# A transformer block on one core: weight blocks of the seven-product pairs loaded along diagonals with one wide addition, and layer norm's steps four blocks at a time

## The chip, the cores and the metric

The kernel runs on one core of a Trainium2 chip. Its time is the device time of one execution in microseconds (us), the median over several runs. A core has an engine for matmuls (PE, TensorE), and beside it VectorE (DVE), ScalarE (ACT), GpSimd (POOL) and SyncE (SP), which here issues nearly all DMAs. Each engine works through a queue of its own in a fixed order; an instruction that has to wait holds up all that stand behind it on that engine.

## The reference

One layer over 256 tokens of width 4096, in float32:

```
xn   = RMSNorm(x)
q, k, v, z_a, a_c, g_c, z_c = split(xn @ w_in)          # 7 x 2048 columns
y_a  = RMSNorm(chunked_attention(q, k, v)) * silu(z_a)  # 16 heads of 128
u    = causal_depthwise_conv_31(a_c * sigmoid(g_c))
y_c  = RMSNorm(silu(layer_norm(u)) @ w_pw + b_pw) * silu(z_c)
h    = x + [y_a, y_c] @ w_out
h    = h + sigmoid(RMSNorm(h) @ w_gate + b) * (p @ w_ple)
out  = RMSNorm(h)
```

Nearly all of the work is in the products with `w_in` (4096 x 14336), `w_pw` (2048 x 2048), `w_out` and `w_gate` (4096 x 4096 each).

## The kernel before

**How a product is tiled.** A float32 product is made of three matmuls on numbers cut into a high and a low part (fp32r): high by high, low by high, high by low. Weights stream from HBM; the activations stay on the core as 128 x 128 blocks. `mixed_product` computes 256 tokens by two blocks of 512 columns. It goes over K in *pairs* of two 128-row blocks, 16 pairs for K = 4096. A plain pair takes 8 block products, so 24 matmuls of 128x512. A pair with a star in the order table (`dense`, `early`, `early_six` and so on) is a *seven-product pair*: a Strassen-like scheme with 7 block products, 21 matmuls. Call the four 128x512 weight blocks of a pair B00, B01 (upper rows, left and right column block) and B10, B11 (lower rows). The scheme needs the sums

```
ua = [B00 + B01, B01 + B11]
ub = [ua0 + B11, ua0 + B11 + B10]
```

beside the blocks B00, B01, B10, B11 themselves. There are 130 such pairs in the program.

**What each engine does for a pair.** SP issues two DMAs of 512 KB into tiles `wt`, of which there are 5 buffers; tile `w0` holds B00 and B01, tile `w1` holds B10 and B11 (L405, through `two_columns`). ACT makes the high parts: `wh` from `wt`, `uh` from `ua` and from `ub` (L204). DVE makes the low parts `wl`, `ul` (L205) and the sums: two additions of 512 elements for `ua` (L428, L429), two for `ub` (L432, L433). For a seven-product pair the low parts are `wl` of B00 alone (128x512, since B01 enters sums only), `wl` of all of `w1` (128x1024), `ul` of `ua` and `ul` of `ub` (128x1024 each). PE then takes P1 (B00), P5 and P7 (`ua`), P2 (B10), P3 (B11), P6 and P4 (`ub`), L372. The banks P2, P3, P4 and one more are called `acc`, the four others `acc_P`.

**What sets the order.** The kernel is written pair by pair; a scheduler then interleaves the instructions on each engine's queue, and every queue is fixed when the program is built. Small pieces of other work lie in a list `later`; `fill(n)` after each pair emits the next n of them. In the first half these are the taps of the convolution (`conv_tap`, L682 and L678, 496 DVE instructions of at most 128x256), then layer norm (`layer_norm_swish`): the mean, subtracting it (`center`, L760, 16 DVE instructions of 128x256), squares, the variance, scaling (L793, 16 of 128x256) with a Silu on ACT after each (L794), and cutting into high and low (L805).

**The products in order of time** in the profile: four of the convolution's input and gate with attention's first products between them (to about 860 us), the pointwise product and attention's end (about 890 to 965), the four of z_a and z_c (to about 1330), four of `w_out` (to about 1670), four of `w_gate` (to the end).

Of the kernel before, what the change touches and what calls it, by code (L numbers as in the profile page):

```python
# [10 lines left out]
F32 = mybir.dt.float32  # L11
# [5 lines left out]
P = 128  # L17
NB = 512
# [7 lines left out]
def hybrid_block(  # L26
# [71 lines left out]

    def two_columns(w, kb, col, apart):

        rows = w[kb * P : (kb + 1) * P, :]
        return bass.AP(
            tensor=rows.tensor, offset=rows.offset + col,
            ap=[list(rows.ap[0]), [apart, 2], [1, NB]],
        )

    w_first = [wpool.tile([P, 2, NB], F32, tag="w", name="wt") for _ in range(2)]
# [91 lines left out]
    def parts_of(wt, kc, tiles=None):  # L199
        if tiles is None:  # L200
            tiles = part_tiles()
        wh, wl = tiles
        made = (
            nc.scalar.copy(wh[:, :kc, :], wt[:, :kc, :]),  # L204
            nc.vector.tensor_tensor(  # L205
                wl[:, :kc, :], wt[:, :kc, :], wh[:, :kc, :].bitcast(F32), ALU.subtract
            ),
        )
        return (wh, wl), made
# [119 lines left out]
    def mixed_product(  # L329
# [67 lines left out]
        for n, (pair, seven) in enumerate(order):  # L397
# [5 lines left out]
            for k in range(2):  # L403
                wt = wpool.tile([P, 2, NB], F32, tag="w", name="wt")
                nc.sync.dma_start(wt, two_columns(w, 2 * pair + k, col, apart))  # L405
                wts.append(wt)
# [16 lines left out]
            w0, w1 = wts  # L423
# [4 lines left out]
            plus(ua[:, 0], w0[:, 0], w0[:, 1])  # L428
            plus(ua[:, 1], w0[:, 1], w1[:, 1])  # L429
            uah, ual = pair_parts(ua)  # L430
            w1h, w1l = parts_of(w1, 2)[0]
            plus(ub[:, 0], ua[:, 0], w1[:, 1])  # L432
            plus(ub[:, 1], ub[:, 0], w1[:, 0])  # L433
            ubh, ubl = pair_parts(ub)
# [296 lines left out]
    def layer_norm_swish():  # L731
# [59 lines left out]
        def swish(c, i):  # L791
            cv, b = conv[c], 4 * c + i
            nc.vector.tensor_tensor(cv[:, i, :], cv[:, i, :], st["rs"], ALU.mult)  # L793
            nc.scalar.activation(  # L794
                cv[:, i, :], cv[:, i, :], AF.Silu,
                scale=ln_g[:, b : b + 1], bias=ln_b[:, b : b + 1],
            )
# [9 lines left out]
        n = len(conv)  # L807
        rest = [lambda: None] * 4
# [487 lines left out]
```

## Time and profile before

| | us |
|---|---|
| runs | 2048.33, 2048.42, 2051.77 |
| median | 2048.42 |
| span of the profiled execution (first to last instruction) | 2049.8 |

The profile is of one more execution; no other time than its span is recorded of it. Times in the trace are us from the span's start. In a row of grouped instructions the columns after the count are busy time, mean duration of one in ns, and the idle time of the engine just before them with what ended it. In a row of windows each engine has its busy time and the number of its instructions; then follow the clock granted to TensorE (1.00 is full), the share of time that the core's 16 DMA engines were busy, and GB/s. In a timeline row the start and the duration come first and, in brackets, how long the engine sat idle before and what it waited for. Durations of neighbouring instructions overlap a little: the distance from one start to the next is what an instruction takes of the engine.

### The profile page before, as it was taken

To read this page: it belongs to the slowest core of one execution; us is meant where nothing else is said; L and a number is where in the kernel's file an instruction comes from. 1 tells how busy PE (TensorE), PEld (TensorE's weight loads), DVE (VectorE), ACT (ScalarE), POOL (GpSimd) and SP (SyncE) were. 2 spreads that over 40 slices of the span, in tenths; PEclk is the share of its full clock that TensorE was granted. 3 is DMA by queue.
4 is the path that set the end of the run, shared out by engine and by line. 5 is a ranking of instruction groups with operands and counts; after the bars stand their busy time and mean duration, and the time that the engine had idled before them with its cause. 6 is when DMAs were issued, how large, how long until landed. Compare 5 with 4: busy or idle time off the path is not lost.

```text
span 2049.8 us, 26039 instructions
## 1 busy us (share of the span) xinstructions
PE 2021.3 (99%) x9082; PEld 1652.6 (81%) x9082; DVE 1944.7 (95%) x2784; ACT 1196.2 (58%) x1543; POOL 8.1 (0%) x19
## 2 busy tenths in 40 slices
PE   9999999999899999999999999999999999999997
PEld 7888888888678888877888888888888888888876
DVE  7999999989999999988899999999999999999998
ACT  7655545655555544576565656676565666655555
POOL 0000000000000000000000000000000000000000
PEclk9999999999999999999999999999999999999998
DMA  8666666566665665754666566676666656666765
GB/s 284 195 195 205 201 192 203 166 198 184 194 187 170 200 184 184 222 164 168 196 217 206 191 218 196 217 241 208 212 200 202 205 188 209 200 219 206 235 207 178
DMA packets 153662, 412.30 MB, mean 201 GB/s; under 512 B 12974, under 2 KB 16190, under 8 KB 153530
## 3 DMA queue, kind: packets, MB, share of 16 engines
q1 hardware_dynamic: 152880, 409.80, 62.7%
q8 instruction: 71, 1.16, 0.2%
q10 hardware_dynamic: 650, 0.84, 0.1%
q14 instruction: 61, 0.50, 0.1%
HBM read 406.39 MB, written 4.19 MB: 200 GB/s over the span
## 4 chain that ended last, share of the span: by engine, by line
PE 87%; DVE 8%; issue 2%; DMA 1%; ACT 1%; SPq 0%; POOL 0%; POOLq 0%; ACTq 0%; DVEq 0%
PE acc L372 68%; PE acc_P L372 15%; DVE wl L205 3%; DVE cv L682 1%; DVE ul L205 1%; PE tmp_ps L170 1%; DMA wt<-in_w_in_dram 1%; PE acc L218 1%; DVE ub L433 0%; DVE ub L432 0%; PE tmp_ps L835 0%; PE tmp_ps L851 0%; DVE ua L428 0%; PE tmp_ps L869 0%; DVE ua L429 0%
## 5 line engine op out<-in xcount | busy, mean ns | idle before, releaser
L372 PE MATMUL acc<-wh,big_t 128*128 128x512 f32 x4196 | 1296.4, 392 | 4.0 <-DVE wh L563 1.6
L204 ACT CAST wh<-wt 128x1024 fp32r<-128x1024 f32 (+1 forms) x737 | 711.9, 977 | 552.3 <-PE acc L372 408.0
L372 PEld LDWEIGHTS acc<-wh,big_t 128*128 128x128 f32 x4196 | 784.2, 188 | 168.5 <-ACT big_t L156 2.4
L205 DVE TENSOR_TENSOR wl<-wt,wh 128x1024 fp32r<-128x1024 f32 (+1 forms) x737 | 821.0, 1125 | 32.3 <-ACT wh L204 28.9
L372 PE MATMUL acc<-wl,big_t 128*128 128x512 f32 x2098 | 804.0, 391 | 2.0 <-DVE wl L205 1.8
L372 PEld LDWEIGHTS acc<-wl,big_t 128*128 128x128 f32 x2098 | 393.0, 188 | 87.1 <-DVE wl L205 5.7
L682 DVE SCALAR_TENSOR_TENSOR cv<-uT,dw,cv 128x255 f32<-128x255 f32 (+22 forms) x480 | 213.1, 463 | 1.0
L204 ACT CAST uh<-ub 128x1024 fp32r<-128x1024 f32 x130 | 136.9, 1053 | 125.5 <-DVE ub L433 105.1
L204 ACT CAST uh<-ua 128x1024 fp32r<-128x1024 f32 x130 | 137.1, 1054 | 84.9 <-DVE ua L429 79.6
L205 DVE TENSOR_TENSOR ul<-ub,uh 128x1024 fp32r<-128x1024 f32 x130 | 158.7, 1221 | 8.1 <-ACT uh L204 6.9
L372 PE MATMUL acc_P<-uh,big_t 128*128 128x512 f32 x528 | 161.7, 393 | 0.0
L205 DVE TENSOR_TENSOR ul<-ua,uh 128x1024 fp32r<-128x1024 f32 x130 | 158.6, 1220 | 0.9 <-ACT uh L204 0.2
L372 PEld LDWEIGHTS acc_P<-uh,big_t 128*128 128x128 f32 x528 | 97.4, 188 | 24.3 <-ACT uh L204 5.0
L428 DVE TENSOR_TENSOR ua<-wt 128x512 f32<-128x512 f32 x130 | 89.3, 687 | 21.8 <-DMA wt<-in_w_in_dram 15.0
L372 PE MATMUL acc_P<-ul,big_t 128*128 128x512 f32 x264 | 101.1, 394 | 1.0 <-DVE ul L205 1.0
L429 DVE TENSOR_TENSOR ua<-wt 128x512 f32<-128x512 f32 x130 | 89.1, 685 | 2.3 <-DMA wt<-in_w_in_dram 1.3
L433 DVE TENSOR_TENSOR ub<-ub,wt 128x512 f32<-128x512 f32 x130 | 89.1, 686 | 0.8
L432 DVE TENSOR_TENSOR ub<-ua,wt 128x512 f32<-128x512 f32 x130 | 89.1, 685 | 0.3
L372 PE MATMUL acc<-uh,big_t 128*128 128x512 f32 x260 | 80.6, 390 | 0.0
L372 PE MATMUL acc_P<-wh,big_t 128*128 128x512 f32 x260 | 80.6, 389 | 0.0
L372 PE MATMUL acc_P<-uh,comb_t 128*128 128x512 f32 x228 | 70.1, 392 | 0.2
L372 PEld LDWEIGHTS acc_P<-ul,big_t 128*128 128x128 f32 x264 | 49.2, 188 | 15.2 <-DVE ul L205 4.9
(240 smaller groups left out, 1367.4 us busy)
## 6 DMA issues: line engine op xcount, KB each, us to landing
wt<-in_w_in_dram SPq DMA_DIRECT2D x447, 512.0 KB, 4.2
wt<-in_w_out_dram SPq DMA_DIRECT2D x128, 512.0 KB, 4.2
wt<-in_w_ple_gate_dram SPq DMA_DIRECT2D x128, 512.0 KB, 4.1
wt<-in_w_pw_dram SPq DMA_DIRECT2D x32, 512.0 KB, 4.6
hc<-in_x_dram SPq DMA_DIRECT2D x8, 512.0 KB, 5.2
wt<-in_w_ple_dram SPq DMA_DIRECT2D x8, 512.0 KB, 4.7
xin<-in_x_dram SPq DMA_DIRECT2D x7, 512.0 KB, 7.9
out_dram<-hc SPq DMA_DIRECT2D x12, 256.0 KB, 2.4
```

Of the source, the lines that this page charges most:

```text
L170: nc.tensor.transpose(pt[:, i * T + h * P : i * T + (h + 1) * P], src[:, h, b] if len(src.shape) == 4 else src[:, h, b * P : (b + 1) * P], ...
L204: nc.scalar.copy(wh[:, :kc, :], wt[:, :kc, :]),
L205: nc.vector.tensor_tensor(wl[:, :kc, :], wt[:, :kc, :], wh[:, :kc, :].bitcast(F32), ALU.subtract),
L218: nc.tensor.matmul(acc, a, b[:, k, :], start=kb == 0 and kind == 0, stop=kb == kblocks - 1 and kind == 2,)
L372: nc.tensor.matmul(banks[name], a, b, start=name not in begun, stop=final and ends[name] == n and kind == 2 and not (left and name in "P2 ...
L428: plus(ua[:, 0], w0[:, 0], w0[:, 1])
L429: plus(ua[:, 1], w0[:, 1], w1[:, 1])
L432: plus(ub[:, 0], ua[:, 0], w1[:, 1])
L433: plus(ub[:, 1], ub[:, 0], w1[:, 0])
L682: nc.vector.scalar_tensor_tensor(cv[:, i, PAD - k :], uT[:, i, : T + k - PAD], dw[:, b, k : k + 1], cv[:, i, PAD - k :], ALU.mult, ALU.add,)
```

## The change

For a seven-product pair the two tiles now hold diagonals: `even` holds B00 and B11, `odd` holds B01 and B10. Both additions of `ua` become one of 1024 elements, `even` plus B01 repeated. `even` is cut into high and low whole (128x1024); of `odd` only B10 is (128x512). `ub` takes B11 from `even` and B10 from `odd`. On PE, P3 moves ahead to the second place and P2 stands after P7. The DMAs of a starred pair read two blocks of 128 rows by 512 columns that lie diagonally; where the two column blocks are neighbours (z_a, z_c, v, `w_pw`, `w_out`, `w_gate`: 194 transfers) a row was one run of 4 KB before and is two runs of 2 KB now. In layer norm the subtraction of the mean and the scaling are one instruction of 128x1024 for four blocks, and the list `later` is four entries shorter.

```diff
+    def diagonal(w, kb, col, apart, other):
+        down = P * w.ap[0][0]
+        return two_blocks(w, kb, col + (apart if other else 0), down + (-apart if other else apart))
...
-                nc.sync.dma_start(wt, two_columns(w, 2 * pair + k, col, apart))
+                src = diagonal(w, 2 * pair, col, apart, k) if seven else two_columns(w, 2 * pair + k, col, apart)
+                nc.sync.dma_start(wt, src)
...
-            w0h, w0l = parts_of(w0, 1)[0]
-            plus(ua[:, 0], w0[:, 0], w0[:, 1])
-            plus(ua[:, 1], w0[:, 1], w1[:, 1])
+            evh, evl = parts_of(even, 2)[0]
+            plus(ua, even, odd[:, :1].to_broadcast([P, 2, NB]))
             uah, ual = pair_parts(ua)
-            w1h, w1l = parts_of(w1, 2)[0]
-            plus(ub[:, 0], ua[:, 0], w1[:, 1])
-            plus(ub[:, 1], ub[:, 0], w1[:, 0])
+            odh, odl = part_tiles()
+            nc.scalar.copy(odh[:, 1], odd[:, 1])
+            nc.vector.tensor_tensor(odl[:, 1], odd[:, 1], odh[:, 1].bitcast(F32), ALU.subtract)
+            plus(ub[:, 0], ua[:, 0], even[:, 1])
+            plus(ub[:, 1], ub[:, 0], odd[:, 1])
...
-            add("P1", block(k0, 0), (w0h[:, 0], w0l[:, 0]), n, True)
+            add("P1", block(k0, 0), (evh[:, 0], evl[:, 0]), n, True)
+            add("P3", s_of(3), (evh[:, 1], evl[:, 1]), n, True)
             add("P5", s_of(1), (uah[:, 0], ual[:, 0]), n, True)
             add("P7", s_of(0), (uah[:, 1], ual[:, 1]), n, True)
-            add("P2", block(k1, 0), (w1h[:, 0], w1l[:, 0]), n, True)
-            add("P3", s_of(3), (w1h[:, 1], w1l[:, 1]), n, True)
+            add("P2", block(k1, 0), (odh[:, 1], odl[:, 1]), n, True)
...
-        def center(c, i):
-            cv = conv[c]
-            nc.vector.tensor_tensor(cv[:, i, :], cv[:, i, :], st["mu"], ALU.subtract)
+        def center(c):
+            add(conv[c], conv[c], every("mu"), ALU.subtract)
...
-            nc.vector.tensor_tensor(cv[:, i, :], cv[:, i, :], st["rs"], ALU.mult)
+            if i == 0:
+                add(cv, cv, every("rs"), ALU.mult)
...
-            later.extend(partial(center, c, i) for i in range(4))
-            later.append(partial(square, c))
+            later.extend((partial(center, c), nothing, nothing, partial(square, c)))
```

**Place A: DVE in the last product of the convolution's input (about 519 to 527 us), at its last starred pair (10\*); `ul_4581` and `ul_4557` belong to the starred pair ahead of it.** Numbers after names tell the buffers of this build apart. Before:

```order
L205 TENSOR_TENSOR wl_4618<-wt_4611,wh_4617 128x512
L682 SCALAR_TENSOR_TENSOR cv_4017<-uT_4004,dw_126,cv_4017 128x248
L205 TENSOR_TENSOR ul_4581<-ub_4563,uh_4580 128x1024
L682 SCALAR_TENSOR_TENSOR cv_4017<-uT_4004,dw_126,cv_4017 128x247
L428 TENSOR_TENSOR ua_4615<-wt_4611 128x512
L682 SCALAR_TENSOR_TENSOR cv_4017<-uT_4004,dw_126,cv_4017 128x246
L429 TENSOR_TENSOR ua_4615<-wt_4611,wt_4613 128x512
L682 SCALAR_TENSOR_TENSOR cv_4017<-uT_4004,dw_126,cv_4017 128x245
L205 TENSOR_TENSOR wl_4628<-wt_4613,wh_4627 128x1024
```

The same place now:

```order
L212 TENSOR_TENSOR wl_4594<-wt_4587,wh_4593 128x1024
L212 TENSOR_TENSOR ul_4557<-ub_4540,uh_4556 128x1024
L691 SCALAR_TENSOR_TENSOR cv_3998<-uT_3985,dw_126,cv_3998 128x248
L436 TENSOR_TENSOR ua_4591<-wt_4587,wt_4589 128x1024
L691 SCALAR_TENSOR_TENSOR cv_3998<-uT_3985,dw_126,cv_3998 128x247
L440 TENSOR_TENSOR wl_4603<-wt_4589,wh_4602 128x512
```

The wide `wl` has moved ahead of `ua`, the narrow one behind it, and two of the taps that stood ahead of the end of `ua` have gone further back.

**Place B: DVE in the last product of `w_out` (about 1595 to 1602 us), where two pairs meet.** Before:

```order
L433 TENSOR_TENSOR ub_13901<-ub_13901,wt_13894 128x512
L428 TENSOR_TENSOR ua_13987<-wt_13983 128x512
L205 TENSOR_TENSOR wl_13952<-wt_13947,wh_13951 128x1024
L205 TENSOR_TENSOR ul_13919<-ub_13901,uh_13918 128x1024
L205 TENSOR_TENSOR wl_13968<-wt_13949,wh_13967 128x1024
L205 TENSOR_TENSOR wl_13990<-wt_13983,wh_13989 128x512
L429 TENSOR_TENSOR ua_13987<-wt_13983,wt_13985 128x512
```

Now:

```order
L442 TENSOR_TENSOR ub_13782<-ub_13782,wt_13775 128x512
L212 TENSOR_TENSOR wl_13832<-wt_13827,wh_13831 128x1024
L212 TENSOR_TENSOR ul_13799<-ub_13782,uh_13798 128x1024
L212 TENSOR_TENSOR wl_13848<-wt_13829,wh_13847 128x1024
L212 TENSOR_TENSOR wl_13870<-wt_13863,wh_13869 128x1024
L436 TENSOR_TENSOR ua_13867<-wt_13863,wt_13865 128x1024
```

The first half of the next pair's `ua` (L428) stood ahead of the pair's own `ul` and two `wl`; the whole `ua` (L436) now stands behind them, about where its second half stood, and needs both transfers.

**Place C: DVE in a z product, at a starred pair, a plain one and the next starred one.** Before, from the instruction that frees a buffer (the transfer `wt_10694` goes into the buffer that `wt_10577` leaves) to the first that needs the new block:

```order
L205 TENSOR_TENSOR wl_10596<-wt_10577,wh_10595 128x1024
L205 TENSOR_TENSOR ul_10624<-ua_10615,uh_10623 128x1024
L205 TENSOR_TENSOR wl_10618<-wt_10611,wh_10617 128x512
L432 TENSOR_TENSOR ub_10616<-ua_10615,wt_10613 128x512
L433 TENSOR_TENSOR ub_10616<-ub_10616,wt_10613 128x512
L428 TENSOR_TENSOR ua_10698<-wt_10694 128x512
```

Now the transfer `wt_10607` (an `odd` tile) goes into the buffer that `wt_10523` (an `even` tile) leaves:

```order
L212 TENSOR_TENSOR wl_10530<-wt_10523,wh_10529 128x1024
L442 TENSOR_TENSOR ub_10528<-ub_10528,wt_10525 128x512
L212 TENSOR_TENSOR ul_10545<-ub_10528,uh_10544 128x1024
L440 TENSOR_TENSOR wl_10539<-wt_10525,wh_10538 128x512
L436 TENSOR_TENSOR ua_10609<-wt_10605,wt_10607 128x1024
```

One instruction of 512 elements fewer lies between the two ends.

More of the change, by code (lines that the diff above doesn't have):

```diff
@@ L97, in hybrid_block, with two_blocks @@
     x_first = act.tile([P, NH, NB], F32, tag="act", name="xin")
-    def two_columns(w, kb, col, apart):
+    def two_blocks(w, kb, col, apart):
         rows = w[kb * P : (kb + 1) * P, :]
@@ L105, in two_columns @@
         )
+    two_columns = two_blocks
+    def diagonal(w, kb, col, apart, other):
+        down = P * w.ap[0][0]
+        return two_blocks(w, kb, col + (apart if other else 0), down + (-apart if other else apart))
     w_first = [wpool.tile([P, 2, NB], F32, tag="w", name="wt") for _ in range(2)]
@@ L422, in mixed_product @@
                 banks.update(helper)
-            w0, w1 = wts
+            even, odd = wts
             ua = upool.tile([P, 2, NB], F32, tag="u", name="ua")
@@ L756, in total, with every @@
                 add(st["s"], st["s"], conv[c], ALU.add)
-        def center(c, i):
-            cv = conv[c]
-            nc.vector.tensor_tensor(cv[:, i, :], cv[:, i, :], st["mu"], ALU.subtract)
+        def every(stat):
+            return st[stat].rearrange("q (o t) -> q o t", o=1).to_broadcast([P, 4, T])
+        def center(c):
+            add(conv[c], conv[c], every("mu"), ALU.subtract)
         def square(c):
@@ L807, in layer_norm_swish @@
         n = len(conv)
-        rest = [lambda: None] * 4
+        nothing = lambda: None
+        rest = [nothing] * 4
         later.extend(partial(total, c) for c in range(n))
```

## The prediction

> **What bounds the kernel now.** I read the head of the page first, then the busy time by stages, then what PE waited for. The head:
>
> ```profile
> span 2049.8 us, 26039 instructions
> PE 2021.3 (99%) x9082; PEld 1652.6 (81%) x9082; DVE 1944.7 (95%) x2784; ACT 1196.2 (58%) x1543; POOL 8.1 (0%) x19
> ```
>
> PE is busy 99% of the span and DVE 95%. An average hides where the one or the other decides, so here are six stages (PE, PEld, DVE, ACT and POOL busy, then clock, DMA share, GB/s):
>
> ```profile
> 20.00:448.00 428.00, 427.77 (x1946) 352.76 (x1945) 408.91 (x641) 241.79 (x315) 1.32 (x2) 1.00 0.64 200
> 448.00:614.00 166.00, 159.91 (x696) 127.37 (x695) 165.19 (x256) 89.53 (x101) 0.31 (x1) 1.00 0.61 187
> 614.00:862.00 248.00, 247.11 (x1126) 202.38 (x1126) 242.36 (x380) 126.30 (x154) 0.31 (x1) 1.00 0.62 191
> 862.00:967.00 105.00, 101.44 (x480) 80.21 (x479) 90.61 (x167) 72.31 (x139) 2.07 (x3) 1.00 0.51 171
> 967.00:1590.00 623.00, 622.27 (x2769) 513.39 (x2769) 589.61 (x751) 379.94 (x457) 0.69 (x1) 1.00 0.64 208
> 1590.00:2016.00 426.00, 424.90 (x1895) 347.25 (x1894) 413.68 (x536) 262.99 (x340) 0.69 (x1) 1.00 0.64 208
> ```
>
> PE's idle time is the stage's length less its first figure: 0.2, 6.1, 0.9, 3.6, 0.7 and 1.1 us, 12.6 in all. **That is the most that any relief of DVE can bring**, since the matmuls stay: the change has as many as before, at a granted clock that is already 1.00. In one stage DVE decides: from 448 to 614 it is busy 165.2 of 166 us while PE idles 6.1. Everywhere else PE is full with DVE at 86 to 98%. What ended PE's idle time, over the span:
>
> ```profile
> PE acc_P L372 <- ACT uh L204: 4.8, 4, 2.4
> PE acc L372 <- DVE wl L205: 1.8, 4, 0.6
> PE acc_P L372 <- DVE ul L205: 1.7, 2, 1.0
> ...
> PE acc L372 <- DVE y_c L985: 1.1, 1, 1.1
> PE tmp_ps L869 <- ACT s L862: 0.9, 2, 0.7
> PE acc L372 <- DVE y_c L987: 0.6, 1, 0.6
> ```
>
> A few single events, then, of which the change can touch those that hang on `uh`, `ul` and `wl`.
>
> **The merged addition.** What goes and what comes, by the groups of DVE:
>
> ```profile
> L428 DVE TENSOR_TENSOR ua<-wt 128x512 f32<-128x512 f32 x130 | 89.3, 687 | 21.8 <-DMA wt<-in_w_in_dram 15.0 <-DMA wt<-in_w_out_dram 5.5 <-DMA wt<-in_w_ple_gate_dram 1.1
> L429 DVE TENSOR_TENSOR ua<-wt 128x512 f32<-128x512 f32 x130 | 89.1, 685 | 2.3 <-DMA wt<-in_w_in_dram 1.3 <-DMA wt<-in_w_out_dram 1.1
> ```
>
> The means, 687 and 685 ns, overlap with the next instruction; what counts is the distance of starts, in three rows that follow each other:
>
> ```profile
> 854.52 1.22 DVE L205 TENSOR_TENSOR wl<-wt,wh 128x1024 fp32r<-128x1024 f32 x1
> 855.65 0.68 DVE L429 TENSOR_TENSOR ua<-wt 128x512 f32<-128x512 f32 x1
> 856.25 0.69 DVE L432 TENSOR_TENSOR ub<-ua,wt 128x512 f32<-128x512 f32 x1
> ```
>
> A 128x1024 operation takes 1.13 us of DVE, a 128x512 one 0.60. Two of the narrow for one of the wide save 2 x 0.60 - 1.13 = 0.07 us, times 130 pairs 9.1 us. The low parts only change places (one wide and one narrow `wl` before and after), so do ACT's casts. The new addition reads B01 twice, a repeated operand that no row shows; between no gain (1.20, two narrow ones) and 1.13 I take 1.13, the wide subtraction being the nearest row: it also reads two float32 streams.
>
> **Layer norm.** The 16 scalings of 128x256 (the 16 subtractions are alike):
>
> ```profile
> 877.65 1.10 DVE L793 TENSOR_TENSOR cv<-cv,rs 128x256 f32<-128x256 f32 x3
> 878.66 0.68 DVE L470 TENSOR_TENSOR z<-acc_P,z 128x512 f32<-128x512 f32 x1
> ```
>
> Three in 1.01 us, so four in 1.35; one of 1024 for 1.13 saves 0.22, eight times 1.7 us. The scaling lies between 862 and 967, where DVE is busy only 90.6 of 105 us: nothing there waits for its capacity, and I count zero. DVE thus loses 10.8 us of work in all, and PE can use little of it.
>
> **What of it reaches PE: place A.** The two largest waits of PE, both on `uh`, the cast of `ua`:
>
> ```profile
> 525.10 1.19 PE L372 MATMUL acc_P<-uh,comb_x 128*128 128x512 f32 x4 [2.38 <-ACT uh L204]
> 529.75 0.74 PE L372 MATMUL acc_P<-uh,comb_x 128*128 128x512 f32 x2 [1.63 <-ACT uh L204]
> ```
>
> On DVE a tap of the convolution between the two halves of `ua` takes 0.39 us:
>
> ```profile
> 522.25 0.68 DVE L428 TENSOR_TENSOR ua<-wt 128x512 f32<-128x512 f32 x1
> 522.85 0.46 DVE L682 SCALAR_TENSOR_TENSOR cv<-uT,dw,cv 128x246 f32<-128x246 f32 x1
> 523.24 0.68 DVE L429 TENSOR_TENSOR ua<-wt 128x512 f32<-128x512 f32 x1
> ```
>
> DVE runs almost without a pause from 448 on, so PE's waits are its arrears: six starred pairs up to there save 6 x 0.07 = 0.4 us. The order adds to it. From the start of `wl` to the end of `ua`, by the rows of place A, there lay one wide operation, three narrow ones and three taps, 1.13 + 3 x 0.60 + 3 x 0.39 = 4.1 us; now three wide ones and one tap, 3 x 1.13 + 0.39 = 3.8. That is 0.3 more. I take **-0.7**; the bounds are 0 and all of the stage's 6.1.
>
> **Place B.** Here DVE stood still at the first half of the next pair's `ua`, and what PE needed stood behind it:
>
> ```profile
> 1597.96 0.69 DVE L428 TENSOR_TENSOR ua<-wt 128x512 f32<-128x512 f32 x1 [1.72 <-DMA wt<-in_w_out_dram]
> 1599.70 1.22 DVE L205 TENSOR_TENSOR ul<-ub,uh 128x1024 fp32r<-128x1024 f32 x1
> 1600.98 0.50 PE L372 MATMUL acc_P<-ul,big_t 128*128 128x512 f32 x1 [0.98 <-DVE ul L205]
> ```
>
> Now `ua` stands behind that `ul`, so the wait no longer holds it up: **-1.0**, bounds 0 and -1.7 (all that PE waits for `ul`).
>
> **The new wait.** In exchange `ua` waits for both transfers. Behind it stand `wl` and `ul` of this and the next pair, for which PE waits. At place C the way from the freed buffer to `ua` was 1.13 + 3 x 0.60 = 2.9 us of DVE work and is 1.13 + 2 x 0.60 = 2.3 now, against a transfer's median of 4.1 to 4.2 us:
>
> ```profile
> wt<-in_w_in_dram SPq DMA_DIRECT2D x447, 512.0 KB, 4.2
> wt<-in_w_ple_gate_dram SPq DMA_DIRECT2D x128, 512.0 KB, 4.1
> ```
>
> So about 0.6 us more of waiting at such a pair. Its cover is PE's stock of finished parts, and the longest such wait of before shows how far it reaches:
>
> ```profile
> 1139.65 0.69 DVE L428 TENSOR_TENSOR ua<-wt 128x512 f32<-128x512 f32 x1 [2.97 <-DMA wt<-in_w_in_dram]
> 1136.00:1160.00 24.00, 24.00 (x106) 19.56 (x105) 20.99 (x24) 15.41 (x17) 0.00 (x0) 1.00 0.62 205
> ```
>
> DVE stood 2.97 us and PE did not miss a moment (24.00 of 24.00). I count **+0.5** for a place where the stock is smaller, as at B; bounds 0 and the rival below.
>
> **Transfers of 2 KB runs instead of 4 KB**, 194 of them. A stretch with 2 KB runs only and one with 4 KB:
>
> ```profile
> 100.00:250.00 150.00, 149.78 (x665) 122.44 (x664) 148.96 (x230) 79.81 (x89) 0.31 (x1) 1.00 0.64 198
> 1100.00:1180.00 80.00, 80.00 (x352) 65.67 (x351) 75.85 (x91) 48.46 (x53) 0.00 (x0) 1.00 0.64 207
> ```
>
> The same share carries 198 GB/s and 207: 4.5% more DMA time on those transfers, 0.2 us of 4.2, at 64% load. Zero, at most the 0.2 us on top of the new wait. The Trainium skill, "Perfetto Trace Analysis", section DMA Optimizations, holds that batching 2 KB into 4 or 8 KB can improve throughput dramatically, which speaks against this edit. By that rule the 194 transfers would grow by much more than 0.2 us and the time would go the way of the slower rival below; the trace agrees on the direction and shows 4.5%.
>
> **PE's order and layer norm's handover.** P3 now needs only `even`: six matmuls instead of three stand ahead of the first that needs `ua`, at 24.00 / 106 = 0.23 us each (the row above at 1136) 1.4 us instead of 0.7. I count zero where PE is full. The first Silu of a tile waits 1.13 us for its scaling instead of 0.34. The Silus after it show why that costs nothing lasting, six in 3.05 us:
>
> ```profile
> 884.20 3.05 ACT L794 ACTIVATE cv<-cv,prm 128x256 f32<-128x256 f32 x6
> ```
>
> Sixteen of them take ACT 8 us; four wide scalings are through in 4 x 1.13 = 4.5 us, so only the first waits, 0.8 us. The same page of the Trainium skill, section Optimizing Scalar/DVE Operations, says that where an engine is not saturated but makes others wait, breaking instructions up may let work finish sooner: by it layer norm's half of the change goes the wrong way. The sum by it would be 0.8 us higher for the one Silu and 3.2 for all four tiles, both still within 0.2% of before.
>
> **The sum:** -0.7 - 1.0 + 0.5 = -1.2 us. The profiled execution spans 2049.8, 1.4 over the median of 2048.42; against its own span that is 2048.6, against the median **2047.2 us**.
>
> **Rivals.**
>
> *Faster: DVE's arrears vanish.* If the taps that stand further back at place A relieve that stage as a whole, its 6.1 us go, and with all the waits on `ul` (1.7) the time is 2048.4 - 7.8 = 2040.6. For it: PE's waits of that stage hang on two pairs. Against it: DVE is busy 165.2 of 166 us there, and the taps still have to be done before the stage ends; moving them moves the wait. Chance 0.26.
>
> *Slower: `ua` at the head of the queue waits for the second transfer.* In each of the twelve products with z, `w_out` and `w_gate`, one starred pair has the short way of place C. If PE's stock is as small there as at B, where a wait of 1.72 cost PE 0.98 us, twelve of these cost 12 x 0.98 = 11.8, less 1.7 from above: 2058.5; half as often, 2052.6. It decides from a wait of about 1.7 us at a pair. Against it: the 2.97 us at 1139.65 that cost nothing, and that `ua` stands further back now. Chance 0.18, for 2053 to 2059.
>
> *The wide addition is no cheaper than two.* Then DVE gains nothing from it, 0.4 us of the sum goes: 2047.6. It is inside my forecast.
>
> **How the numbers follow.** The forecast, PE full and a microsecond either way, gets 0.56 and by itself spans 2044.5 to 2052. A measurement of this kernel can tell about 0.2%, 4.1 us, from no change: 2044.3 to 2052.5. Faster by more has 0.26, slower by more 0.18, the same 0.56. The range, 2040 to 2054, takes in the faster rival and the lower part of the slower one.
>
> **What would show it.** Right: 130 additions of 128x1024 at about 1.22 us each and a start distance of 1.13; DVE busy about 11 us less; PE still 99%; between 448 and 614 PE idle 5 to 6 us; no wait of PE on `ul` near 1600. Idle time of DVE ahead of `ua` about as large as the 24 us of L428 and L429 now, with waits of 2 to 3 us at single pairs. Wrong: PE idle in many small pieces between 967 and 2016 behind a waiting `ua` (the slower rival), or PE idle below 2 us between 448 and 614 (the faster one), or an addition that takes much more than 1.22 us.

## The result: slower by 0.7%

The changed kernel takes 2063.81 us (median of 4 runs, 2060.95 to 2065.70) against 2049.09 us for the kernel before (4 runs, 2048.33 to 2051.77): a ratio of 1.0070 with a 95% interval from 1.0057 to 1.0082. In a second measurement, beside the experiments, it came to 1.0081 (1.0068 to 1.0095). The forecast, 2047.2 us with a range to 2054, was wrong in its sign and too narrow.

The head of the changed kernel's page, its six stages and PE's waits, for comparison with the rows of before (span 2049.8):

```profile
span 2062.4 us, 25913 instructions
PE 2030.6 (98%) x9082; PEld 1654.3 (80%) x9082; DVE 1936.0 (94%) x2630; ACT 1192.8 (58%) x1543; POOL 15.5 (1%) x19
```

```profile
20.00:448.00 428.00, 426.91 (x1939) 351.29 (x1938) 406.54 (x620) 239.27 (x312) 8.27 (x2) 1.00 0.65 199
448.00:614.00 166.00, 162.01 (x692) 128.39 (x691) 162.51 (x244) 88.86 (x100) 0.30 (x1) 0.98 0.59 184
614.00:862.00 248.00, 247.45 (x1131) 202.94 (x1130) 241.30 (x360) 125.95 (x153) 1.31 (x3) 1.00 0.62 192
862.00:967.00 105.00, 101.74 (x471) 79.63 (x469) 87.35 (x144) 72.80 (x139) 1.06 (x1) 0.98 0.51 164
967.00:1590.00 623.00, 617.30 (x2735) 506.25 (x2736) 579.79 (x692) 373.60 (x451) 1.06 (x1) 1.00 0.66 207
1590.00:2016.00 426.00, 423.85 (x1884) 345.82 (x1883) 410.77 (x502) 258.95 (x337) 0.69 (x1) 1.00 0.66 207
```

```profile
PE acc L379 <- DVE wl L212: 5.3, 6, 1.5
PE acc_P L379 <- ACT uh L211: 2.7, 6, 1.2
PE acc L379 <- ACT wh L211: 2.3, 1, 2.3
PE acc L379 <- DVE wl L440: 2.0, 2, 1.5
PE acc L379 <- DVE y_c L997: 1.4, 1, 1.4
```

DVE did become lighter, by 8.7 us, and PE still waits more: the stage from 967 to 1590 has 5.7 us of idle PE where it had 0.7, and the stages at 448 and 862 have a granted clock of 0.98 where it was 1.00. Idle time alone hides the clock, so I also set the two executions side by side by matmul. Both have 9082 matmuls, and the n-th, counted from nought, starts at (us):

```
n                  1200   2000   2600   3800    4600    6400    7050    7600    9000
before            268.9  444.1  587.6  853.7  1032.6  1434.4  1582.6  1703.1  2022.0
changed           269.5  445.2  589.8  853.9  1036.7  1439.1  1593.2  1715.2  2035.1
later by            0.7    1.1    2.2    0.2     4.1     4.6    10.6    12.0    13.0
```

So the loss has **two places**: around 900 us (3.9 us between the 3800th and 4600th matmul), and the products with `w_out` from 1439 on (7.4 us between the 6400th and 7600th). Single executions of one kernel differ by some microseconds (2060.95 to 2065.70 above), so the sizes below come from medians of repeated runs, and the trace only says where.

**The first place** is on ACT. After the scale `rs` of the layer norm, its queue held (changed kernel, timeline of ACT):

```profile
879.31 1.28 ACT L806 ACT_TABLE_LOAD   x1
880.61 3.56 ACT L806 ACTIVATE cv<-cv,prm 128x256 f32<-128x256 f32 x7
884.07 0.71 ACT L501 ACTIVATE z<-z,r_x 128x512 f32<-128x512 f32 x1
884.68 2.07 ACT L806 ACTIVATE cv<-cv,prm 128x256 f32<-128x256 f32 x4
886.65 1.33 ACT L501 ACTIVATE z<-z,r_x 128x512 f32<-128x512 f32 x2
887.88 2.06 ACT L806 ACTIVATE cv<-cv,prm 128x256 f32<-128x256 f32 x4
889.84 1.03 ACT L211 CAST wh<-wt 128x1024 fp32r<-128x1024 f32 x1
```

and PE stood until that cast came:

```profile
890.93 1.91 PE L379 MATMUL acc<-wh,big_t 128*128 128x512 f32 x6 [2.33 <-ACT wh L211]
```

Fifteen Silus (7 + 4 + 4) stand ahead of the weight cast. In the kernel before it was eleven (3, 2 and 6, with the same three operations on `z`):

```profile
879.87 1.59 ACT L794 ACTIVATE cv<-cv,prm 128x256 f32<-128x256 f32 x3
881.37 0.71 ACT L492 ACTIVATE z<-z,r_x 128x512 f32<-128x512 f32 x1
881.98 1.08 ACT L794 ACTIVATE cv<-cv,prm 128x256 f32<-128x256 f32 x2
882.97 1.33 ACT L492 ACTIVATE z<-z,r_x 128x512 f32<-128x512 f32 x2
884.20 3.05 ACT L794 ACTIVATE cv<-cv,prm 128x256 f32<-128x256 f32 x6
887.16 1.03 ACT L204 CAST wh<-wt 128x1024 fp32r<-128x1024 f32 x1
```

Part of the 3.9 us is the granted clock, which fell behind this wait (last section).

**The second place** is DVE at `ua`. The timeline of DVE late in the second product with `w_out`, only the rows ahead of which it idled:

```profile
1473.43 1.23 DVE L212 TENSOR_TENSOR ul<-ub,uh 128x1024 fp32r<-128x1024 f32 x1 [0.57 <-ACT uh L211]
1475.59 1.23 DVE L436 TENSOR_TENSOR ua<-wt 128x1024 f32<-128x1024 f32 x1 [0.93 <-DMA wt<-in_w_out_dram]
...
1483.75 1.23 DVE L212 TENSOR_TENSOR ul<-ub,uh 128x1024 fp32r<-128x1024 f32 x1 [1.20 <-ACT uh L211]
...
1486.93 1.23 DVE L436 TENSOR_TENSOR ua<-wt 128x1024 f32<-128x1024 f32 x1 [1.35 <-DMA wt<-in_w_out_dram]
```

and PE behind it:

```profile
1490.07 0.50 PE L379 MATMUL acc<-wl,big_t 128*128 128x512 f32 x1 [1.45 <-DVE wl L212]
```

No single wait is long, but four of them, 4.05 us, fall within 15 us, and PE's stock of finished parts (what DVE and ACT have made ready ahead of it) runs out. In the kernel before, four waits of DVE in the third product, 3.75 us together, lay spread over 30 us (1538.7 to 1568.5), and PE did not wait. The same as at 1490 happens at 1574 (PE waits 1.18 us) and 1659 (1.29), once in each of the two products that follow. These three waits are 3.9 us of the 7.4; the rest lies in shorter pauses between matmuls.

### The profile page after: what moved, and what is told of

It is laid out like the page before. It is cut to its first block, busy times and chain, and to the rows that moved or that the text cites. A ratio compares the mean times of both kernels' runs of the same rounds, so it can differ in the third digit from the quotient of the medians.

```text
span 2062.4 us, 25913 instructions
## 1 busy us (share of the span) xinstructions
PE 2030.6 (98%) x9082; PEld 1654.3 (80%) x9082; DVE 1936.0 (94%) x2630; ACT 1192.8 (58%) x1543; POOL 15.5 (1%) x19
## 4 chain that ended last, share of the span: by engine, by line
PE 44%; DVE 7%; issue 2%; DMA 2%; ACT 1%; POOLq 0%; POOL 0%; DVEq 0%; ACTq 0%
PE acc L379 33%; PE acc_P L379 9%; DVE wl L212 2%; DVE ul L212 2%; DMA wt<-in_w_out_dram 1%; DVE ua L436 1%; PE acc L225 1%; PE tmp_ps L177 1%; DMA wt<-in_w_in_dram 0%; ACT uh L211 0%; DVE ub L442 0%; DVE ub L441 0%; DMA wt<-in_w_ple_dram 0%; ACT wh L211 0%; DVE wl L440 0%
## 5 line engine op out<-in xcount | busy, mean ns | idle before, releaser
L211 ACT CAST wh<-wt 128x1024 fp32r<-128x1024 f32 x607 | 634.5, 1051 | 399.3 <-PE acc L379 298.6
L212 DVE TENSOR_TENSOR wl<-wt,wh 128x1024 fp32r<-128x1024 f32 x607 | 732.6, 1217 | 37.8 <-ACT wh L211 34.8
L691 DVE SCALAR_TENSOR_TENSOR cv<-uT,dw,cv 128x255 f32<-128x255 f32 (+27 forms) x480 | 210.3, 461 | 0.9
L436 DVE TENSOR_TENSOR ua<-wt 128x1024 f32<-128x1024 f32 x130 | 158.5, 1219 | 29.5 <-DMA wt<-in_w_out_dram 14.6
L212 DVE TENSOR_TENSOR ul<-ub,uh 128x1024 fp32r<-128x1024 f32 x130 | 158.4, 1219 | 15.3 <-ACT uh L211 14.8
L439 ACT CAST wh<-wt 128x512 fp32r<-128x512 f32 x130 | 80.5, 620 | 132.0 <-PE acc L379 114.4
L440 DVE TENSOR_TENSOR wl<-wt,wh 128x512 fp32r<-128x512 f32 x130 | 88.8, 683 | 0.4 <-ACT wh L439 0.2
```

Source lines behind the costliest of these rows:

```text
L212: nc.vector.tensor_tensor(wl[:, :kc, :], wt[:, :kc, :], wh[:, :kc, :].bitcast(F32), ALU.subtract),
L436: plus(ua, even, odd[:, :1].to_broadcast([P, 2, NB]))
L439: nc.scalar.copy(odh[:, 1], odd[:, 1])
L440: nc.vector.tensor_tensor(odl[:, 1], odd[:, 1], odh[:, 1].bitcast(F32), ALU.subtract)
L691: nc.vector.scalar_tensor_tensor(cv[:, i, PAD - k :], uT[:, i, : T + k - PAD], dw[:, b, k : k + 1], cv[:, i, PAD - k :], ALU.mult, ALU.add,)
```

## The experiments

Each kernel was timed against the kernel before on the same chip; the ratio is to that, with its 95% interval. Not all groups ran on the same chip, so two kernels of different groups are compared by what each loses against its own kernel before.

### The two halves apart

`ln_only` is the kernel before with the layer norm's part of the change, `pair_only` the changed kernel with the layer norm of before.

> The kernel before with the layer norm's wide subtractions and scalings alone; the starred pairs load and add as before. In the changed kernel the same matmul (counted from the start) comes 4.1 us later than before at 1033 us, and had come only 0.2 us later at 853 us; in between lies a PE wait of 2.33 us on a weight cast that stood on ACT behind seven Silus in a row (3.56 us). Theory L, the wide scaling makes four blocks ready at once, so that Silus fill ACT's queue ahead of a cast: 2051 to 2053 us, with a PE wait of about 2 us on ACT near 890 us again. Rival, that stage lost because the starred pairs ahead of it ran late: 2048.5 to 2049.5 us and no such wait.

> The changed kernel with the layer norm block by block as before: the diagonal loads, the wide addition and the new order of the products alone. If the pairs carry the loss in the w_out passes (7.4 us between 1440 and 1680 us) and the slow loss behind them (1.4 us), and the layer norm the 4 us around 900 us: 2057 to 2060 us. If the stage around 900 us is lost to the pairs too: 2062 to 2065 us. If the two parts only hurt together: under 2055 us.

Measured: `ln_only` **1.0015** (1.0006 to 1.0024), 2051.40 us; `pair_only` **1.0043** (1.0031 to 1.0056), 2057.65 us. Both halves lose. `ln_only` has the wait of 2.32 us on a cast again. The changed kernel once more beside its parts:

> The changed kernel once more, on the same chip as its parts. The parts alone give 1.0043 (pairs) and 1.0015 (layer norm), together 1.0058; the changed kernel gave 1.0070 with an interval from 1.0057. If the parts only add up: 1.0050 to 1.0066. If they hurt each other around 900 us, where the pairs run late into the stage that the layer norm's Silus hold up: 1.0068 to 1.008.

Measured 1.0081 (1.0068 to 1.0095), against 1.0058 for the sum of the two halves. They may hurt each other by some 0.001 to 0.002, but with the intervals of all three this is not shown.

### Layer norm: not the scaling but the list

The expectation of `ln_only` blamed the wide scaling, which makes four blocks ready for Silu at once. To test it, each wide operation alone in the kernel before:

```diff
 ln_scale, in swish:
-            nc.vector.tensor_tensor(cv[:, i, :], cv[:, i, :], st["rs"], ALU.mult)
+            if i == 0:
+                add(cv, cv, every("rs"), ALU.mult)
 ln_center, in the list:
-            later.extend(partial(center, c, i) for i in range(4))
-            later.append(partial(square, c))
+            later.extend((partial(center, c), nothing, nothing, partial(square, c)))
```

> The kernel before with the layer norm's scalings by rs four blocks wide and the subtractions block by block as before. Theory L (four blocks ready at once line up Silus on ACT ahead of a weight cast): the whole loss of the layer norm's part, ratio 1.001 to 1.002, 2050 to 2052 us, with seven Silus in a row on ACT and PE waiting about 2.3 us for the cast near 888 us. If the shifted list of pieces (subtractions and squares) does it: ratio 0.9995 to 1.0005.

> The kernel before with the layer norm's subtractions of mu four blocks wide and the scalings block by block as before. Theory L: no loss, ratio 0.9990 to 1.0005, no PE wait of 2 us for a cast near 888 us; with 0.9 us less DVE work it might gain up to 0.5 us. If the shifted list does it: ratio 1.001 to 1.002, 2050 to 2052 us.

Measured: `ln_scale` 1.0003 (0.9994 to 1.0011), `ln_center` **1.0013** (1.0004 to 1.0022). **The theory fell**: the scaling costs nothing that the interval shows, the subtraction about all of it. ACT's timeline in `ln_center`, where the scalings are narrow, has the long run of Silus all the same (7 + 8):

```profile
875.94 1.28 ACT L796 ACT_TABLE_LOAD   x1
877.24 3.56 ACT L796 ACTIVATE cv<-cv,prm 128x256 f32<-128x256 f32 x7
880.70 1.94 ACT L492 ACTIVATE z<-z,r_x 128x512 f32<-128x512 f32 x3
882.54 4.03 ACT L796 ACTIVATE cv<-cv,prm 128x256 f32<-128x256 f32 x8
886.48 1.03 ACT L204 CAST wh<-wt 128x1024 fp32r<-128x1024 f32 x1
```

What the wide subtraction changes besides DVE is the list `later`: four pieces for a tile instead of five, four tiles, four pieces fewer. Everything behind them in the list is handed out four pieces earlier, and four pieces of that part are four Silus. So the next kernel has both wide operations, but a list of the old length:

```diff
-            later.extend((partial(center, c), nothing, nothing, partial(square, c)))
+            later.extend((partial(center, c), nothing, nothing, nothing, partial(square, c)))
```

> The kernel before with both wide operations of the layer norm, but with the list of pieces at its old length: one more empty piece between the subtraction of a tile and its squares, five per tile as before and not four. On ACT eleven Silus again stand ahead of the weight cast near 888 us where the wide subtractions alone had fifteen. Theory S (the shifted list is the layer norm's loss): ratio 0.9990 to 1.0006, no PE wait of 2 us there. Rival (the wide subtraction itself holds something up): ratio 1.001 to 1.002.

Measured 1.0002 (0.9993 to 1.0011). ACT has eleven Silus ahead of the cast again (3 + 6 + 2):

```profile
878.91 1.59 ACT L797 ACTIVATE cv<-cv,prm 128x256 f32<-128x256 f32 x3
880.41 0.71 ACT L492 ACTIVATE z<-z,r_x 128x512 f32<-128x512 f32 x1
881.02 3.05 ACT L797 ACTIVATE cv<-cv,prm 128x256 f32<-128x256 f32 x6
883.98 1.32 ACT L492 ACTIVATE z<-z,r_x 128x512 f32<-128x512 f32 x2
885.21 1.08 ACT L797 ACTIVATE cv<-cv,prm 128x256 f32<-128x256 f32 x2
886.19 1.03 ACT L204 CAST wh<-wt 128x1024 fp32r<-128x1024 f32 x1
```

One empty piece per tile removes the whole loss of this half, so the shorter list is the cause. That it acts through the 2 us of four Silus ahead of one cast is what the timelines show at this place; no kernel moved those Silus alone.

### The pairs: held tiles, both tiles needed, smaller pieces

The diagonals do three things to a pair's loads: the first tile is held until `ub`, the first addition needs both tiles, and rows come in pieces of 2 KB. Each was put into the kernel before by itself.

```diff
 hold:
-            plus(ub[:, 0], ua[:, 0], w1[:, 1])
+            plus(ub[:, 0], ua[:, 1], w0[:, 0])
 both:
-            plus(ua[:, 0], w0[:, 0], w0[:, 1])
             plus(ua[:, 1], w0[:, 1], w1[:, 1])
+            plus(ua[:, 0], w0[:, 0], w0[:, 1])
 pieces:
-                nc.sync.dma_start(wt, two_columns(w, 2 * pair + k, col, apart))
+                src = two_columns(w, 2 * pair + k, col, apart)
+                if seven:
+                    src = two_columns(w, 2 * pair + k, col + apart, -apart)
+                nc.sync.dma_start(wt[:, ::-1] if seven else wt, src)
```

> The kernel before, with the first sum of the second source read from the first tile: ub0 = ua1 + w0[0] in place of ua0 + w1[1], the same numbers added in another order. No instruction is added, no load changes; the first tile of a starred pair is now held until ub's first addition, as the even tile is in the changed kernel, and both tiles come free late. Theory H (buffers that come free later make the loads issue later, and an addition waits for them at the head of DVE's queue): 2054 to 2061 us, SP's waits named by ub's first addition in place of ua's second one. Theory B (the wide addition is late because it needs both tiles) and theory P (pieces of 2 KB land later): 2048 to 2050 us.

> The kernel before with ua's two additions in the other order: the one that needs both tiles comes first, so that the head of a pair's additions needs both transfers, as in the changed kernel; no tile is held longer, no load changes. Theory B (waiting for both transfers at the head of the queue is the loss): 2054 to 2061 us, DVE's waits for loads clearly over the 21.8 us of before. Theories H (buffers held longer) and P (pieces of 2 KB): 2048 to 2050.5 us.

> The kernel before with the two blocks of each starred pair's row loaded in the other order into the tile's two halves turned round, so that the same data land in the same places but in pieces of 2 KB. Order of all engines is as before. Median landing in the changed kernel is 4.5 us for the w_out and w_ple_gate transfers against 4.2 and 4.1 before. Theory P (pieces of 2 KB land later, and that starves DVE): landing medians up by 0.2 to 0.4 us and 2051 to 2055 us. Rival (later landing came from later issues that bunch together): landing medians as before and 2047.5 to 2050 us.

Measured: `hold` 1.0003 (0.9994 to 1.0012), `both` **1.0029** (1.0017 to 1.0040), `pieces` **1.0034** (1.0021 to 1.0047). Holding alone is not it, though the loads did wait for the later release; SP's waits in `hold`, where the kernel before had `ua L429: 121.0, 58` and `ub L433: 140.9, 47`:

```profile
SPq L405 <- DVE ub L432: 290.7, 91, 7.7
```

`pieces` leaves the order on every engine as it was, and lands the same data in the same places, as two turned round pieces a row. DVE's waits for loads at the first half of `ua` (L431 in this kernel) grew from 15.0 and 5.5 us to:

```profile
DVE ua L431 <- DMA wt<-in_w_in_dram: 25.6, 23, 3.5
DVE ua L431 <- DMA wt<-in_w_out_dram: 9.0, 10, 1.5
```

The same two edits together:

> The kernel before with both single changes together: the addition that needs both tiles first (alone 2054.66 us, ratio 1.0029) and the starred rows in pieces of 2 KB (alone 2055.51 us, ratio 1.0034); no wide addition, no diagonal, no other order of the products. If the two add up: ratio 1.0063, 2061 to 2062 us. If they spend the same slack of the loads and overlap: ratio 1.0035 to 1.005, 2055 to 2058 us, and then the two alone give the whole of what the pairs of the changed kernel cost (1.0043 and, with narrow additions, 1.0049).

Measured **1.0111** (1.0098 to 1.0125), 2070.03 us: neither overlap nor sum, but 1.8 times the sum. A reading that fits, and no more, is that PE's stock covers either delay for the most part and is used up with both. It also suggests that the changed pairs, at 1.0043, have something that gives time back.

### What gives it back

In the changed pairs P3 needs only `even`, so two products, six matmuls, can run before `ua` is needed. `order_p` is `pair_only` with P3 behind P2 again. `two_adds_p` is `pair_only` with the wide addition made as two of 512.

> The changed kernel's pairs (layer norm as before; 2057.65 us, 1.0043) with the products in the order of before: P1, P5, P7, P2, P3, so that one product and not two can run on the even tile's parts before ua's are needed. Theory O (the early P3 gives PE a stock that covers part of the wait for both tiles): clearly slower, 2062 to 2070 us. Rival (the order of the products changes nothing, the diagonals land better than the turned round pieces): 2055 to 2060 us.

> The changed kernel's pairs (layer norm as before, 2057.65 us) with the wide addition made as two additions of 512 again; loads by diagonals, holding of the tiles and the need for both tiles stay. Two additions of 512 take 1.20 us of DVE where the wide one takes 1.13, so this adds some 9 us of DVE work over 130 pairs. If the time follows DVE's work in the places where DVE is behind: 2058 to 2063 us. If the wide addition is itself part of the loss, as one instruction that can't start on what has landed and that the order puts elsewhere: 2051 to 2056 us, near the 2054.66 us of the kernel before with the both-tiles addition first.

Measured: `order_p` **1.0075** (1.0062 to 1.0087), 2062.21 us; `two_adds_p` 1.0049 (1.0036 to 1.0063), 2057.62 us. Against the kernel before on their own chips `pair_only` loses 8.8 us, `order_p` 14.8 and `two_adds_p` 9.9. The early P3 is worth some 6 us. The wide addition, for which the tiles were rearranged, is worth some 1 us by these medians, which the intervals don't tell from nothing, though it saves some 9 us of DVE's work. This fits that PE waits for what DVE waits for, rather than for DVE's work. In `order_p` the longest wait of `ua` in `w_out` is 4.2 us, and PE waits more there (PE's waits from 1440 to 1700 us):

```profile
PE acc_P L379 <- DVE ul L212: 3.4, 2, 1.7
PE acc L379 <- DVE wl L212: 3.3, 2, 2.9
```

### Two repairs that failed

`pair_ub_early` writes both additions of `ub` directly behind `ua`, to free the tiles sooner. `behind_p` puts `ua` behind the last subtraction of the pair before, so that no `ul` can stand behind a waiting `ua`.

```diff
 behind_p:
-            plus(ua, even, odd[:, :1].to_broadcast([P, 2, NB]))
+            with ExitStack() as queued:
+                if sums:
+                    queued.enter_context(tc.issue_after(sums[-1].ins))
+                plus(ua, even, odd[:, :1].to_broadcast([P, 2, NB]))
```

> The changed kernel's pairs (layer norm as before, 2057.65 us) with both of ub's additions written directly behind ua, ahead of ua's parts and the odd block's parts, so that both tiles may come free sooner. In the kernel before, a longer hold of one tile alone gave 2050.0 us, no loss that the interval shows. Theory H (late release adds to the loss once both tiles are needed): 2053 to 2056 us, SP's waits for ub shorter. Rival (the need for both tiles is all): 2056.5 to 2060 us.

> The changed kernel's pairs (layer norm as before, 2057.65 us), with one edge of order more: the wide addition of a pair is put on DVE behind the last subtraction (ul of ub) of the pair before. Theory Q: part of the loss is that ua waits for its transfers at the head of DVE's queue while the last parts of the pair before, which PE needs first, stand behind it: 2052 to 2056 us. Rival: what DVE loses is the waiting itself, whatever stands behind, since buffers and transfers set when ua can run: 2057 to 2060 us, and the sum of ua's waits for loads (24.5 us in the pairs alone) about as large.

Measured: `pair_ub_early` 1.0052 (1.0040 to 1.0065), no better than `pair_only`. `behind_p` **1.0108** (1.0094 to 1.0122), 2069.47 us, far worse than either expectation. `ua`'s waits for loads did not shrink (28.9 us against 24.5 in `pair_only`), and DVE's waits at `ul` grew from 16.8 us. A reading that was not tested: `ua` starts later, and with it the cast `uh` on ACT, for which `ul` then waits:

```profile
DVE ul L212 <- ACT uh L211: 25.1, 40, 1.2
```

### In which products

From each load's issue and landing in the trace, the starred loads alone (their means, us; 45 to 56 loads in each group have a landing; `w_ple_gate` is the kernel's name of `w_gate`):

```
                        before   changed   pair_only   pieces   pieces_out   across_out
w_in from 967 us on       4.07      4.11        4.02     4.50         4.08         3.81
w_out                     4.32      4.83        4.68     4.61         4.64         4.82
w_ple_gate                4.21      4.69        4.64     4.36         4.47         4.65
```

The diagonals of `w_in` land no later than its rows; those of `w_out` and `w_ple_gate` 0.4 to 0.5 us later. So I put the changed pairs into one group of products and left the other as before.

```diff
+        across = w is w_in0          # across_in; "is not" in across_out
...
-                src = diagonal(...) if seven else two_columns(...)
+                src = diagonal(...) if seven and across else two_columns(...)
```

(and for a starred pair the loads, additions and order of products of the one or of the other kernel).

> Diagonals, wide addition and new order only in the products with w_in; w_pw, w_out and w_ple_gate load rows and add as before (layer norm as before). In the changed pairs the starred loads of w_in land no later than before (mean 4.02 us against 4.07 between 967 and 1320 us), those of w_out and w_ple_gate do (4.68 and 4.64 against 4.32 and 4.21), and the changed pairs fall behind from 1485 us on. Theory D (the diagonals of w_out and w_ple_gate land late and carry the loss): ratio 0.999 to 1.0012, 2046 to 2050 us. Rival (the need for both tiles costs alike everywhere): about half of the pairs' loss, 1.002 to 1.003, 2051 to 2054 us.

> The mirror image: diagonals, wide addition and new order only in the products with w_pw, w_out and w_ple_gate; those with w_in as before (layer norm as before). Theory D: ratio 1.0035 to 1.005, 2055 to 2058 us, PE's waits between 1440 and 1690 us as in the changed kernel. Rival (costs alike everywhere): 1.0015 to 1.0025, 2050.5 to 2053 us.

Measured: `across_in` 1.0006 (0.9997 to 1.0015), 2047.77 us; `across_out` **1.0045** (1.0031 to 1.0058), 2056.18 us, as much as the pairs lose everywhere. PE's waits from 1440 to 1700 us, `across_out` first, `across_in` second:

```profile
PE acc L380 <- DVE wl L212: 4.2, 3, 1.7
```

```profile
PE acc_P L380 <- DVE ul L212: 0.6, 1, 0.6
```

Last, the two single edits again, in these products alone:

> The kernel before with the addition that needs both tiles first, in the products with w_pw, w_out and w_ple_gate alone; loads as before. The same edit everywhere gave 1.0029, and diagonals in these products alone 1.0045. If the need for both tiles is what costs there: ratio 1.002 to 1.004. If later landing is: 0.9995 to 1.001. If it takes both together: 0.9995 to 1.0015 here and under 1.002 in the run beside it.

> The kernel before with the starred rows loaded in turned round pieces of 2 KB in the products with w_pw, w_out and w_ple_gate alone; the order on all engines and the additions as before. The same edit everywhere gave 1.0034, its starred loads of w_out landing 0.29 us later on average (4.61 against 4.32). If later landing is what costs the diagonals: ratio 1.002 to 1.004. If the need for both tiles is: 0.9995 to 1.001. If it takes both together: under 1.002.

Measured: `both_out` 1.0006 (0.9998 to 1.0015), `pieces_out` 1.0013 (1.0004 to 1.0022). Neither alone makes the 1.0045, nor does their sum. Both numbers are what was expected if it takes later landing and the need for both tiles together. But no kernel had both edits in these products alone, and `both_pieces` does not show it for them, since its loss lies elsewhere. How much later than in the kernel before the n-th matmul starts (us, one execution of each):

```
n                  1200   3800   4600   6400   7600   9000
both                2.7    2.5    3.4    3.5    3.4    4.0
pieces             -0.9   -1.2    1.8    4.3    4.8    5.1
both_pieces         1.5    3.7    8.7   19.3   22.1   22.8
across_out         -1.2   -1.5   -1.3   -1.9    4.1    5.0
```

`both_pieces` loses 15.6 us from the 3800th to the 6400th matmul, mostly in the products of z_a and z_c with `w_in`, where the diagonals cost nothing that `across_in` shows, and 2.8 us from there to the 7600th, in `w_out`, where `across_out` loses 6.0. So the single edits say what can delay `ua`, not what delays it in the changed `w_out`.

The traces hold a further difference that none of the single edits has. A starred pair's second load in `w_out` is issued 1.63 us after its first in the kernel before (mean), 1.64 in `both_out`, 1.63 in `pieces_out` and 1.89 in `hold`, but 3.07 in `pair_only` and 3.11 in `across_out`, and the one addition needs both. In the z products the distance grows too (1.90 to 2.86 us), without a loss. No run has this by itself, so which parts of the change make the 1.0045 stays open, beside the diagonals' later landing (4.82 against 4.64 us in `pieces_out`).

No kernel here is faster than before beyond its interval; the nearest to a gain, `across_in` and `ln_pad`, are the same within theirs.

## Why the prediction was wrong

**The step that failed is the new wait.** It was put at +0.5 us because DVE's wait of 2.97 us at 1139.65 had cost PE nothing; the pairs alone cost 8.8 us, and with diagonals in `w_pw`, `w_out` and `w_gate` alone they cost as much. The wait at 1139.65 was one wait, in a product with `w_in`, with no other within 20 us. In `w_out` shorter waits of `ua` (0.93 and 1.35 us) come together with waits for `uh`, and PE's stock is gone after two pairs. That `ua` waits for loads at the head of the queue is the slower rival's mechanism, and the traces show it in `w_out` (14.6 us where it was 6.6); that the need for the second transfer alone does it is not borne out (`both_out`, 1.0006). Its price, 2058.5 us, is close to the 2057.65 of the pairs alone by luck: it was made of twelve like places, four of them in z products, where `across_in` shows no loss. Its condition was wrong: it was to decide from waits of about 1.7 us, and the longest in `w_out` was 1.6. Waits add up; the single longest one says little. The span that the forecast gave itself, 2044.5 to 2052, follows from no term of the sum.

**Transfers of 2 KB** were put at 0, at most 0.2 us each, from the DMA engines' busy share. That share cannot show it: a packet of 2 KB takes 104 ns and one of 4 KB 202 (means in `before`), nearly the same per byte, and the queue's share did not grow with the packets (`before`, then `pieces`):

```profile
q1 hardware_dynamic: 152880, 409.80, 62.7%
```

```profile
q1 hardware_dynamic: 177712, 409.80, 61.7%
```

What grew is the time from issue to landing, by 0.15 to 0.43 us in `pieces` and 0.5 us in the changed kernel's `w_out` and `w_ple_gate`, and DVE's waits at `ua` grew with it. The size of the pieces alone does not decide that: the diagonals of z come in 2 KB too and land no later (4.11 us against 4.07, and 4.50 in `pieces`). The rule cited from the Trainium skill, "Perfetto Trace Analysis", section DMA Optimizations, pointed the right way where I gave the row's 4.5% the word. It speaks of throughput, though, and that did not change: HBM was read and written at 200 GB/s before and 199 after.

**Layer norm** was put at zero, and costs 1.0013 to 1.0015, about 3 us. I weighed the first Silu's wait for the wide scaling, which by `ln_scale` costs nothing that the interval shows, and passed over the shorter list, which is in the change's description. So the rule cited from the Trainium skill, "Perfetto Trace Analysis", section Optimizing Scalar/DVE Operations, that breaking instructions up may help, gave the right sign for a reason that the runs don't bear out: wide operations with a padded list cost nothing that the interval shows (1.0002).

**The merged addition** was right in size and wrong in worth:

```profile
L436 DVE TENSOR_TENSOR ua<-wt 128x1024 f32<-128x1024 f32 x130 | 158.5, 1219 | 29.5 <-DMA wt<-in_w_out_dram 14.6 <-DMA wt<-in_w_in_dram 13.3 <-DMA wt<-in_w_ple_gate_dram 1.4
```

1219 ns, as the 1220 of the wide subtraction `ul` before; the repeated operand costs nothing. DVE's work shrank by 8.7 us (10.8 forecast), its waits ahead of `ua` grew from 24 us to 29.5, those at `ul` for `uh` from 7.8 to 16.0. The latter are as large in `across_in` (15.1), which loses nothing, so they alone are not what costs.

**Place A** (-0.7) came as idle time and not as time: two shorter waits (1.51 and 1.24 us) replaced the old two, and PE's idle time from 448 to 614 fell from 6.1 to 4.0 us, but the clock dropped (last section), and between the 2000th and the 2600th matmul the changed kernel lost 1.1 us. **Place B** (-1.0) came as forecast: the wait on `ul` near 1600 is gone. It is only small beside the rest. **PE's new order** was put at zero, and is worth some 6 us; without it the changed kernel would be slower still.

## What to carry to other kernels

A wait is hidden or not by what the waiting engine's consumer has in stock at that place; take the cover from the same product, add up all waits that fall close together, and remember that two delays can cost more together than one by one (here 1.0111 against 1.0029 and 1.0034). An edit that loses as much need not lose it in the same place, so compare the traces place by place. Work taken from a busy engine can be worth next to nothing where that engine is waiting for transfers and for another engine's casts. Where a list deals out small pieces of work, its length is part of the schedule: an instruction merged away must leave an empty piece, or everything behind it moves.

## What the hardware did that I had not expected

The granted clock fell after short waits, and not after every longer one. In the changed kernel PE waited 1.51 us at 525.44, and in the 8 us from 526 the clock was 0.57:

```profile
526.00:534.00 8.00, 6.64 (x17) 4.78 (x18) 7.36 (x10) 2.07 (x3) 0.00 (x0) 0.57 0.55 185
```

Two matmuls then take 1.05 us instead of 0.62 (the rows around 501 us of the kernel before):

```profile
527.35 1.05 PE L379 MATMUL acc<-wh,big_t 128*128 128x512 f32 x2
```

In the kernel before, the two waits at this place were 2.38 and 1.63 us, and the clock stayed full:

```profile
524.00:532.00 8.00, 5.27 (x22) 4.05 (x23) 8.00 (x12) 3.15 (x3) 0.00 (x0) 1.00 0.47 134
```

The same halving follows the wait of 2.33 us at 890.93 in the changed kernel, not the wait of 2.32 us of `ln_only` at 887.40. The wait of 2.38 us near 525 us is followed by half clock in `both_out` and `ln_scale`, and by full clock in `before`, `ln_only` and `hold`. Leaving out the end of the program, the clock's records show half clock (0.5) for 3.41 or 6.83 us at a time wherever a trace here has it. The Trainium skill, "TensorE: Matmul & The Clock Gate", Part 1, says that the clock halves after an idle window of about 3.4 us, a window that runs freely. No wait ahead of these stretches is that long, so half clock did not take an idle time of this length; the stretches at half clock are once and twice the page's figure, and a window that runs freely would fit that like waits end differently. No run here tests that. A short wait of PE may thus cost more than its length, and the trace shows the rest in the clock column, not as idle time.

That the diagonals land later in `w_out` and `w_ple_gate` and not in `w_in` has no cause shown here. The two blocks of a diagonal lie 128 rows apart, 2 MB in the former (rows of 16 KB) and 7 MB in the latter (rows of 56 KB). The Trainium skill, "DMA: Bandwidth & Descriptors", section Latency and other measured facts, reports slower copies where the pitch from one partition's row to the next is a large power of two, 164 GB/s at 2 MiB against 207 at 512 KiB, and calls its mechanism an inference; that is another distance than the one between two blocks of one row here, and no run here tests either.
